# A hybrid decoder layer on one core: modulation tiles issued by GpSimd

## The chip, the cores and the metric

The kernel runs on one core of a Trainium2 chip. The time is the device time of one execution in microseconds (us). TensorE (PE), VectorE (DVE), ScalarE (ACT), GpSimd (POOL) and SyncE (SP) each work through a queue of their own in order; semaphores tie them together. DMAs are issued from such a queue: in the kernel before nearly all of them by SP.

## The reference

One layer of a decoder on 256 tokens with 2048 channels, in f32. What matters here:

```python
mod = jax.nn.silu(c) @ w_ada[l] + b_ada[l]                     # (1, 6*2048), w_ada is 2048 x 12288
shift1, scale1, gate1, shift2, scale2, gate2 = jnp.split(mod[:, None, :], N_MOD, axis=-1)
h = rms_norm(x, norm1_gain[l]) * (1 + scale1) + shift1
x = x + gate1 * mixing_sublayer(h, w_in[l], ...)               # three attention branches behind h @ w_in
h = rms_norm(x, norm2_gain[l]) * (1 + scale2) + shift2
x = x + gate2 * swiglu(h, w_ffn_in[l], w_ffn_out[l])
```

`c` is one vector, so the modulation is a product of a vector with a 100 MB matrix.

## The kernel before

**Precise matmuls.** Every weight tile (`raw`, 128 x 1024 f32, 0.5 MB) is loaded by SP, cast by ACT to a rounded part (`whi`, L148), and DVE subtracts to get the rest (`wlo`, L149). `mm3` (L154 to L156) makes three matmuls of each product. There are four buffers each of `raw`, `whi` and `wlo`.

**The modulation** does not run on TensorE. Tiles of `w_ada` are loaded, and DVE multiplies each by one element of silu(c) per partition (`csil`) and adds it up in `ada` (`ada_mac`: L257 for the first tile of a sum, L259 for the others). At the end TensorE transposes the sums (L309), DVE reduces them (L310), and `finish_columns` (L316, L319) adds the bias and makes shift and scale. `make_h` then makes the two parts of the modulated input (ACT L417, DVE L421 and L424).

**Groups.** The 16 chunks of 128 channels of h are made in four groups (3, 4, 4 and 5 chunks), so that the input projection can start with the first three. While TensorE runs the 13 column blocks of the projection for the chunks of one group, the modulation of the next group is summed up (`ada_group`, 16 tiles for the second and the third group, 32 smaller ones for the fourth). Its tiles take turns in the buffers named in `ADA_TAGS`, which the first group uses too. The gate and second-norm segments follow later, in tiles of 128 x 1024 with buffers `AR0`, `AR1` and others (`ada_segment_steps`, L346).

**The opening** (`first_group`, `load_vectors`). SP issues c, three vectors (gains and the bias of the modulation), three of the first group's `w_ada` tiles (L486, 128 x 2 x 384), the first weight tile, x in four parts, the other thirteen `w_ada` tiles, then weight tiles and the second group's tiles. POOL makes the identity and issues seven small vectors. TensorE runs matmuls whose result nobody uses (`keep_warm`, counts in `WARM`) between its first transposes. DVE adds up the sixteen products, the last one in three pieces; a chain of sum, `finish_columns` and `make_h` for each of the three chunks leads to the first matmuls of the projection.

**The order.** A list scheduler sets the order of the instructions on each engine: it goes by priorities (`prio`), data dependences, buffers and its own estimates of when each engine is free; `tc.issue_after` adds an edge. So a change of the issuing engine also changes orders on the other engines. In every queue, a waiting instruction holds up all that stand behind it.

Of the kernel before, what the change touches and what calls it, by code (L numbers as in the profile page):

```python
# [17 lines left out]
P = 128  # L18
# [5 lines left out]
NB = 512  # L24
# [8 lines left out]
RATE_IN, RATE_MID, RATE_FFN = 0.8, 0.6, 0.4  # L33
DEFER = 4
AHEAD = 4000
WARM = (22, 43, 10, 3)
FIN = 13
GROUPS = ((0, 3), (3, 7), (7, 11), (11, 16))
GLA_LEVELS = (1, 2, 4, 8, 16, 32, 64)
# [27 lines left out]
def trunk(ctx: ExitStack, tc: tile.TileContext, I, out):  # L67
    nc = tc.nc
# [14 lines left out]
    def S(tag, shape, dtype=F32):  # L83
        return slot.tile(shape, dtype, tag=tag, name=nm(tag))

    def small(shape, dtype=F32, bufs=8):
        return sp.tile(shape, dtype, tag="tiny", name=nm("tiny"), bufs=bufs)
# [10 lines left out]
    @contextmanager  # L98
    def prio(offset=AHEAD):

        with tc.high_priority(offset=offset):
            start = tc.cur_priority
            yield
            n = tc.cur_priority - start
        tc.cur_priority += n

    state = {"rate": 0.0}
# [84 lines left out]
    def by_chunk(name):  # L192
        return I[name].rearrange("o (k p) -> (o k) p", p=P)
# [14 lines left out]
    rows = S("H6", [P, P])  # L208
    brow = S("H5", [P, P])
# [1 line left out]
    bada = const.tile([P, 96], F32, name="bada")  # L211

    def load_vectors():
        nc.sync.dma_start(rows[16:32, :], by_chunk("norm1_gain"))
        nc.sync.dma_start(brow[0:96, :], by_chunk("b_ada"))
        nc.sync.dma_start(rows[32:48, :], by_chunk("norm2_gain"))
        with tc.issue_after(made):
            for r, name in (
                (ROW_SBQ, "sb_q_gain"),
                (ROW_SBK, "sb_k_gain"),  # L220
                (ROW_DILQ, "dil_q_gain"),
                (ROW_DILK, "dil_k_gain"),
            ):
                nc.gpsimd.dma_start(rows[r : r + 1, :], I[name])
            nc.gpsimd.dma_start(rows[ROW_GB : ROW_GB + 4, :], by_chunk("b_gla_a"))
            nc.gpsimd.dma_start(rows[ROW_GG : ROW_GG + 2, :], by_chunk("gla_out_gain"))
            nc.gpsimd.dma_start(rows[0:16, :], by_chunk("c"))
# [24 lines left out]
    w_ada = I["w_ada"]  # L252

    def ada_mac(acc, raw, k):
        c = csil[:, k : k + 1]
        if k == 0:
            nc.vector.tensor_scalar(acc, raw, c, None, op0=ALU.mult)  # L257
        else:
            nc.vector.scalar_tensor_tensor(acc, raw, c, acc, op0=ALU.mult, op1=ALU.add)  # L259

    ADA_TAGS = ("T4", "T5", "OS0", "OS1", "OS2", "OD")

    mod1 = const.tile([P, 2, KC], F32, name="mod1")

    def ada_group(k0, k1, tags=ADA_TAGS, between=None):

        n = k1 - k0
        sh, sc = mod1[:, 0, k0:k1], mod1[:, 1, k0:k1]
        count = 0
        pieces = -(-n // 4)  # L270
        for i in range(pieces):
            a = k0 + n * i // pieces
            m = k0 + n * (i + 1) // pieces - a
            w = m * P
            acc = S("ada", [P, 2, w])
            for k in range(KC):
                with prio():
                    raw = S(tags[count % len(tags)], [P, 2, w])
                    nc.sync.dma_start(
                        raw,  # L280
                        w_ada[k * P : (k + 1) * P, : 2 * D].rearrange("p (s c) -> p s c", s=2)[:, :, a * P : a * P + w],
                    )
                    with tc.issue_after(state["macs_after"]) if "macs_after" in state else nullcontext():
                        ada_mac(acc, raw, k)
                count += 1
                if k < KC - 1:
                    yield
            if between is not None:
                between()
            with prio():  # L290
                c = slice(a - k0, a - k0 + m)
                sums = small([P, 2, m])
                for j in range(2):
                    turned_sums(sums[:, j, :], acc[:, j, :])
                finish_columns(sums[:, 0, :], sh[:, c], SEG_SHIFT1, a)
                finish_columns(sums[:, 1, :], sc[:, c], SEG_SCALE1, a, ROW_N1)
            yield
        gains[GROUPS.index((k0, k1))] = (sh, sc)
# [4 lines left out]
    def turned_sums(dst, acc, behind=None):  # L303

        n = dst.shape[1]
        ps = misc_bank([P, n, P])
        for i in range(n):
            with tc.issue_after(behind) if behind is not None else nullcontext():
                nc.tensor.transpose(ps[:, i, :], acc[:, i * P : (i + 1) * P], ident)  # L309
        nc.vector.reduce_sum(dst, ps, axis=AX.X)  # L310
# [12 lines left out]
    def araw(shape, dtype=F32):  # L323
        ring["n"] += 1
        return S(ring["tags"][ring["n"] % len(ring["tags"])], shape, dtype)
# [10 lines left out]
    def ada_segment_steps(acc, seg, done):  # L336


        for k in range(KC):
            for j in range(2):  # L340
                while len(macs) >= len(ring["tags"]):
                    mac()
                raw = araw([P, 2 * NB])
                c0 = seg * D + j * 2 * NB
                with prio():
                    nc.sync.dma_start(raw, w_ada[k * P : (k + 1) * P, c0 : c0 + 2 * NB])  # L346
                macs.append((acc, j, k, raw, done if (k, j) == (KC - 1, 1) else None))
                yield

# [51 lines left out]
    def keep_warm(n):  # L401

        ps = acc_bank()
        for _ in range(n):
            state["warm"] = nc.tensor.matmul(ps, ones_r, wide, start=True, stop=True)
# [26 lines left out]
    A = [None] * 13  # L432
# [42 lines left out]
    def first_group():  # L475


        k0, n = GROUPS[0]
        w = n * P
        tags = tuple(f"A{j}" for j in range(9)) + ADA_TAGS  # L480
        raws = []

        def load(ks):
            for k in ks:
                raw = S(tags[k % len(tags)], [P, 2, w])
                nc.sync.dma_start(raw, w_ada[k * P : (k + 1) * P, : 2 * D].rearrange("p (s c) -> p s c", s=2)[:, :, :w])  # L486
                raws.append(raw)

        load(range(0, 3))
        early.extend(load_weights(w_in, 0, 2, orders[0][0] * NB, ahead=False))  # L490
        split = state["split"]
        load_x()
        load(range(3, KC))
        with tc.issue_after(c_turn.ins):
            keep_warm(WARM[0])
        with tc.issue_after(state["warm"].ins):
            turn_vectors()
        with tc.issue_after(state["row_turn"].ins):
            keep_warm(WARM[1])
        norm1()  # L500
        with tc.issue_after(state["turn"].ins):
            keep_warm(WARM[2])
        acc = S("ada", [P, 2, w])
        for k in range(KC - 1):
            with tc.issue_after(split.ins) if k > 3 else nullcontext():
                ada_mac(acc, raws[k], k)
        sh, sc = mod1[:, 0, 0:n], mod1[:, 1, 0:n]
        chunk = lambda q: slice(q * P, (q + 1) * P)

        def last_mac(q):  # L510
            return ada_mac(acc[:, :, chunk(q)], raws[KC - 1][:, :, chunk(q)], KC - 1)

        last_mac(0)
        last_mac(1)
        behind = state["warm"]
        for q in range(n):
            if q == 0:
                sums = misc_bank([P, 2])
                for j in range(2):
                    with tc.issue_after(behind.ins):  # L520
                        behind = column_sum(sums[:, j : j + 1], acc[:, j, chunk(q)])
            else:
                ps = misc_bank([P, 2, P])
                for j in range(2):
                    with tc.issue_after(behind.ins):
                        behind = nc.tensor.transpose(ps[:, j, :], acc[:, j, chunk(q)], ident)
                sums = small([P, 2])
                with tc.issue_after(state["h_lo"].ins):
                    nc.vector.reduce_sum(sums, ps, axis=AX.X)
            finish_columns(sums[:, 0:1], sh[:, q : q + 1], SEG_SHIFT1, q)  # L530
            finish_columns(sums[:, 1:2], sc[:, q : q + 1], SEG_SCALE1, q, ROW_N1)
            if q == 0:
                with tc.issue_after(state["finish"].ins):
                    last_mac(2)
            make_h(q, sh[:, q : q + 1], sc[:, q : q + 1], True)
            if q == 0:
                with tc.issue_after(state["h_first"].ins):
                    early.extend(load_weights(w_in, 2, n, orders[0][0] * NB, ahead=False))
        with tc.issue_after(behind.ins):
            keep_warm(WARM[3])  # L540
        gains[0] = (sh, sc)

    with prio(30000):
# [687 lines left out]
```

## Time and profile before

| | us |
|---|---|
| Median of 3 runs (lowest, highest) | 1619.66 (1618.76, 1620.27) |
| Profiled execution, its own time | 1621.66 |
| Its span in the trace | 1619.90 |
| PE busy | 1604.0 |
| DVE busy | 1118.7 |
| ACT busy | 796.2 |
| POOL busy | 5.3 |
| Transfers | 395.94 MB, mean 244 GB/s |

Busy times are sums over the span; a busy PE includes the unused matmuls of the opening. The granted clock of TensorE is 1.00 in the whole execution. In the views of the profile a row names the line of the kernel, the engine, the tile written and the tiles read; `SPq` and `POOLq` are the DMA issues of those queues. Lines are those of the kernel before; the changed kernel is one line shorter, so that its later lines stand one earlier.

### The profile page before, as it was taken

The page shows a single profiled execution, that of the slowest core. Times are in us where ns is not written, and L with a number is a line of the kernel's source. Part 1 is how long each engine was busy: PE and PEld are TensorE (multiplying, and loading weights), DVE is VectorE, ACT ScalarE, POOL GpSimd, SP SyncE. Part 2 cuts the span into 40 slices and gives each one's busy share as a digit, 9 for nine tenths or more (in the row PEclk, how much of TensorE's full clock was granted, in tenths as well). Part 3 has the DMA queues.
Part 4 walks back from the last instruction along what each step waited for, and adds up shares of the span by engine and source line. Part 5 has one row for each costly group of instructions (what it writes and reads, how often), then busy time and mean ns, then how long its engine had stood idle before and what let it go on. Part 6 is the DMA issues. An engine that isn't in the chain of part 4 may idle for free.

```text
span 1619.9 us, 19947 instructions
## 1 busy us (share of the span) xinstructions
PE 1604.0 (99%) x7341; PEld 1322.8 (82%) x7341; DVE 1118.7 (69%) x1301; ACT 796.2 (49%) x1116; POOL 5.3 (0%) x14
## 2 busy tenths in 40 slices
PE   8999999999999999999999999999999999999998
PEld 7878888788888878888887888888888888888887
DVE  6889995869888687878657566667655555455453
ACT  5654448764875434444446544444434444433332
POOL 1000000000000000000000000000000000000000
PEclk9999999999999999999999999999999999999999
DMA  9999997865868889888766577888666666666663
GB/s 323 340 328 325 330 307 240 275 215 163 288 213 262 298 297 313 309 298 297 242 192 193 167 242 255 276 266 270 199 194 183 193 184 189 188 206 196 207 205 107
DMA packets 194594, 395.94 MB, mean 244 GB/s; under 512 B 12915, under 2 KB 27929, under 8 KB 194497
## 3 DMA queue, kind: packets, MB, share of 16 engines
q1 hardware_dynamic: 194272, 394.67, 75.1%
q8 instruction: 57, 0.93, 0.2%
q14 instruction: 41, 0.33, 0.1%
q0 software_dynamic: 224, 0.01, 0.0%
HBM read 392.53 MB, written 2.10 MB: 244 GB/s over the span
## 4 chain that ended last, share of the span: by engine, by line
PE 89%; DMA 4%; DVE 3%; ACT 2%; issue 1%; SPq 0%; DVEq 0%; ACTq 0%
PE acc L156 28%; PE acc L155 28%; PE acc L154 28%; DMA raw<-w_in 1%; DVE wlo L149 1%; ACT whi L148 1%; PE misc L742 1%; PE misc L1017 1%; DMA AR<-w_ada 1%; DMA A<-w_ada 1%; DMA OS<-w_ada 1%; DVE ada L259 0%; DMA raw<-w_br_gla 0%; PE misc L309 0%; DMA raw<-w_ffn_in 0%
## 5 line engine op out<-in xcount | busy, mean ns | idle before, releaser
L149 DVE TENSOR_TENSOR wlo<-raw,whi 128x1024 fp32r<-128x1024 f32 (+1 forms) x546 | 651.4, 1197 | 436.5 <-ACT whi L148 434.8
L148 ACT CAST whi<-raw 128x1024 fp32r<-128x1024 f32 (+1 forms) x546 | 562.5, 1033 | 713.8 <-PE acc L156 591.4
L155 PE MATMUL acc<-wlo,H 128*128 128x512 f32 x1576 | 615.4, 390 | 1.7 <-DVE wlo L149 1.5
L154 PE MATMUL acc<-whi,H 128*128 128x512 f32 x1576 | 616.2, 391 | 0.5 <-ACT H L417 0.4
L156 PE MATMUL acc<-whi,H 128*128 128x512 f32 x1576 | 615.5, 391 | 0.4 <-DVE H L424 0.4
L155 PEld LDWEIGHTS acc<-wlo,H 128*128 128x128 f32 x1576 | 296.0, 188 | 62.9 <-DVE wlo L149 2.9
L156 PEld LDWEIGHTS acc<-whi,H 128*128 128x128 f32 x1576 | 295.7, 188 | 63.3 <-DVE H L424 1.8
L154 PEld LDWEIGHTS acc<-whi,H 128*128 128x128 f32 x1576 | 295.9, 188 | 61.3 <-ACT H L417 1.3
L154 PE MATMUL acc<-whi,A 128*128 128x512 f32 x312 | 122.0, 391 | 0.3 <-ACT whi L148 0.3
L155 PE MATMUL acc<-wlo,A 128*128 128x512 f32 x312 | 121.5, 389 | 0.8 <-DVE wlo L149 0.8
L156 PE MATMUL acc<-whi,A 128*128 128x512 f32 x280 | 109.0, 389 | 0.0
L259 DVE SCALAR_TENSOR_TENSOR ada<-AR,csil,ada 128x1024 f32<-128x1024 f32 x59 | 75.1, 1277 | 1.2 <-DMA AR<-w_ada 1.2
L155 PEld LDWEIGHTS acc<-wlo,A 128*128 128x128 f32 x312 | 58.6, 188 | 13.1 <-DVE wlo L149 1.1
L154 PEld LDWEIGHTS acc<-whi,A 128*128 128x128 f32 x312 | 58.6, 188 | 12.7 <-ACT whi L148 0.7
L156 PEld LDWEIGHTS acc<-whi,A 128*128 128x128 f32 x280 | 52.5, 188 | 10.9
L154 PE MATMUL acc<-whi,T 128*128 128x512 f32 x120 | 46.7, 389 | 0.0
L155 PE MATMUL acc<-wlo,T 128*128 128x512 f32 x120 | 46.7, 389 | 0.0
L156 PE MATMUL acc<-whi,T 128*128 128x512 f32 x120 | 46.7, 389 | 0.0
L156 PE MATMUL acc<-whi,OS 128*128 128x512 f32 x112 | 43.6, 389 | 0.0
L259 DVE SCALAR_TENSOR_TENSOR ada<-OS,csil,ada 128x1024 f32<-128x1024 f32 (+2 forms) x33 | 35.6, 1077 | 1.5 <-DMA OS<-w_ada 1.3
L461 ACT COPY A<-acc 128x512 f32<-128x512 f32 x50 | 28.9, 586 | 12.5 <-PE acc L156 11.2
L463 DVE TENSOR_TENSOR A<-A,acc 128x512 f32<-128x512 f32 x48 | 31.5, 682 | 2.0 <-PE acc L156 1.8
(337 smaller groups left out, 1214.8 us busy)
## 6 DMA issues: line engine op xcount, KB each, us to landing
raw<-w_in SPq DMA_DIRECT2D x205, 512.0 KB, 5.0
raw<-w_ffn_in SPq DMA_DIRECT2D x176, 512.0 KB, 3.9
raw<-w_ffn_out SPq DMA_DIRECT2D x88, 512.0 KB, 4.7
AR<-w_ada SPq DMA_DIRECT2D x79, 512.0 KB, 4.8
raw<-w_out SPq DMA_DIRECT2D x32, 512.0 KB, 5.0
KC<-w_ada SPq DMA_DIRECT2D x30, 512.0 KB, 5.1
OS<-w_ada SPq DMA_DIRECT2D x16, 512.0 KB, 6.4
raw<-w_br_gla SPq DMA_DIRECT2D x16, 512.0 KB, 7.0
```

The source lines that it names most:

```text
L148: state["cast"] = nc.scalar.copy(hi[:, :n, :], raw[:, :n, :])
L149: state["split"] = nc.vector.tensor_tensor(lo[:, :n, :], raw[:, :n, :], hi[:, :n, :].bitcast(F32), op=ALU.subtract)
L154: nc.tensor.matmul(ps, lh, rh, start=start, stop=False, skip_group_check=seeded)
L155: nc.tensor.matmul(ps, lh, rl, start=False, stop=False, skip_group_check=seeded)
L156: state["mm"] = nc.tensor.matmul(ps, ll, rh, start=False, stop=stop, skip_group_check=seeded)
L259: nc.vector.scalar_tensor_tensor(acc, raw, c, acc, op0=ALU.mult, op1=ALU.add)
L461: nc.scalar.copy(A[b][:, t, :], pss[t])
L463: nc.vector.tensor_add(A[b][:, t, :], A[b][:, t, :], pss[t])
L742: nc.tensor.matmul(ps[:n, h, L:], at(lhs, h, t)[:, :n], at(rhs, h, t)[:, L:], start=True, stop=True)
L1017: nc.tensor.transpose(ps[:, i, :], src[:, i * P : (i + 1) * P], ident)
```

## The change

All `w_ada` tiles but those of the first group are issued by GpSimd instead of SP. Three vectors of the opening are issued by ScalarE instead of SP. The order of the buffers in `ADA_TAGS` is turned by one place (the first group keeps the old order). The unused matmuls are regrouped, 73 in three groups for 78 in four. The third weight chunk of the first block is cast and split behind the second chunk of h instead of the first.

```diff
-WARM = (22, 43, 10, 3)
+WARM = (22, 38, 13)
...
     def load_vectors():
-        nc.sync.dma_start(rows[16:32, :], by_chunk("norm1_gain"))
-        nc.sync.dma_start(brow[0:96, :], by_chunk("b_ada"))
-        nc.sync.dma_start(rows[32:48, :], by_chunk("norm2_gain"))
+        nc.scalar.dma_start(rows[16:32, :], by_chunk("norm1_gain"))
+        nc.scalar.dma_start(brow[0:96, :], by_chunk("b_ada"))
+        nc.scalar.dma_start(rows[32:48, :], by_chunk("norm2_gain"))
...
-    ADA_TAGS = ("T4", "T5", "OS0", "OS1", "OS2", "OD")
+    ADA_TAGS = ("OD", "T4", "T5", "OS0", "OS1", "OS2")
...
     def ada_group(k0, k1, tags=ADA_TAGS, between=None):
...
                     raw = S(tags[count % len(tags)], [P, 2, w])
-                    nc.sync.dma_start(
+                    nc.gpsimd.dma_start(
                         raw,
                         w_ada[k * P : (k + 1) * P, : 2 * D].rearrange("p (s c) -> p s c", s=2)[:, :, a * P : a * P + w],
                     )
...
     def ada_segment_steps(acc, seg, done):
...
-                    nc.sync.dma_start(raw, w_ada[k * P : (k + 1) * P, c0 : c0 + 2 * NB])
+                    nc.gpsimd.dma_start(raw, w_ada[k * P : (k + 1) * P, c0 : c0 + 2 * NB])
...
     def first_group():
...
-        tags = tuple(f"A{j}" for j in range(9)) + ADA_TAGS
+        tags = tuple(f"A{j}" for j in range(9)) + ADA_TAGS[1:] + ADA_TAGS[:1]
...
             make_h(q, sh[:, q : q + 1], sc[:, q : q + 1], True)
-            if q == 0:
-                with tc.issue_after(state["h_first"].ins):
+            if q == 1:
+                state["casts_after"] = state["h_hi"].ins
+                with tc.issue_after(state["h_lo"].ins):
                     early.extend(load_weights(w_in, 2, n, orders[0][0] * NB, ahead=False))
-        with tc.issue_after(behind.ins):
-            keep_warm(WARM[3])
         gains[0] = (sh, sc)
```

## The prediction

> **What bounds the kernel now.** I read the engine shares and the chain of work first. TensorE is the bound:
>
> ```profile
> PE 1604.0 (99%) x7341; PEld 1322.8 (82%) x7341; DVE 1118.7 (69%) x1301; ACT 796.2 (49%) x1116; POOL 5.3 (0%) x14
> PE 89%; DMA 4%; DVE 3%; ACT 2%; issue 1%; SPq 0%; DVEq 0%; ACTq 0%
> ```
>
> So the time is the moment at which PE's real matmuls start to run without a break, plus a fixed amount of PE work, plus the few stalls behind it. The change can only move the start and the stalls. Next I read the windows (columns: window, length, busy time of PE, PEld, DVE, ACT, POOL, granted clock, DMA share, GB/s); the last three were chosen round the stalls that the timeline shows:
>
> ```profile
> 0.00:10.00 10.00, 7.48 (x23) 5.92 (x23) 2.98 (x10) 1.47 (x2) 4.28 (x13) 1.00 0.66 203
> 10.00:20.00 10.00, 10.00 (x45) 7.84 (x44) 5.17 (x7) 8.45 (x23) 0.00 (x0) 1.00 1.04 385
> 20.00:30.00 10.00, 10.00 (x78) 9.39 (x76) 8.78 (x10) 5.27 (x10) 0.00 (x0) 1.00 1.06 376
> 100.00:150.00 50.00, 50.00 (x223) 41.40 (x222) 47.88 (x50) 19.82 (x20) 0.00 (x0) 1.00 0.96 335
> 270.00:284.00 14.00, 13.03 (x71) 10.64 (x70) 9.49 (x14) 11.27 (x20) 0.00 (x0) 1.00 0.85 280
> 318.00:324.00 6.00, 5.49 (x26) 4.29 (x25) 4.46 (x7) 3.35 (x6) 0.00 (x0) 1.00 0.81 262
> 574.00:584.00 10.00, 8.95 (x38) 6.85 (x38) 6.10 (x8) 4.06 (x4) 0.00 (x0) 1.00 0.89 309
> ```
>
> The opening is limited by transfers: 9.64 MB move in 30 us, in the end at 376 GB/s, and the chain of waits passes through them into the last modulation products of the first group:
>
> ```profile
> 18.10 9.32 DMA OS<-w_ada
> 27.52 1.03 DVE ada L259
> 28.57 1.03 DVE ada L259
> 29.62 1.03 DVE ada L259
> 151.92 0.87 PE misc L309 x8
> ```
>
> The timeline gives the landmarks (start, length, engine):
>
> ```profile
> 1.19 0.41 SPq L214 DMA_DIRECT2D H<-norm_gain  x1
> 2.58 1.46 SPq L486 DMA_DIRECT2D A<-w_ada  x3
> 10.85 1.05 ACT L148 CAST whi<-raw 128x1024 fp32r<-128x1024 f32 x1 [7.85 <-DMA raw<-w_in]
> 23.45 2.07 DVE L259 SCALAR_TENSOR_TENSOR ada<-T,csil,ada 128x768 f32<-128x768 f32 x2
> 30.68 0.88 DVE L259 SCALAR_TENSOR_TENSOR ada<-A,csil,ada 128x256 f32<-128x256 f32 x2
> 37.82 0.75 DVE L257 TENSOR_SCALAR ada<-T,csil 128x1024 f32<-128x1024 f32 x1
> 39.76 0.50 PE L155 MATMUL acc<-wlo,H 128*128 128x512 f32 x1
> 50.09 0.39 PE L156 MATMUL acc<-whi,H 128*128 128x512 f32 x1
> 51.45 0.39 PE L156 MATMUL acc<-whi,H 128*128 128x512 f32 x1
> ```
>
> The first group's sixteenth tile is used at 30.68; 7.14 us later DVE starts the second group's first product (L257), and 1.94 us after that, at 39.76, PE runs on. The last two rows are six matmuls apart: 0.2267 us each.
>
> **The change, part by part.** *Three vectors to ScalarE's queue.* SP's first w_ada issue moves from 2.58 to 1.19: the transfers start 1.39 us earlier.
>
> *AR tiles at the very start.* In the built order two gate tiles (128x1024 f32, 0.524 MB each) stand on POOL ahead of the identity, since nothing holds them there; before, they stood at the 169th place of SP's queue. 1.05 MB at 376 GB/s is 2.8 us in a stretch that is limited by transfers. Together: the sixteenth tile, without anything else, at 30.68 - 1.39 + 2.8 = 32.1. DVE's new order (the first weight split ahead of csil) lets the products begin only behind that weight tile, 10.85 + 1.4 = 12.3, plus 3.1 for cast, split and csil; the backlog is worked off before the fourth tile, so this costs nothing.
>
> *POOL's own queue.* It can issue a tile of the second group as soon as a T or OS buffer is free, that is behind the first group's tenth product (23.45 + 1.05 + 1.4 = 25.9), and 1.4 us later its bytes flow, at 27.3. They then run beside the rest of SP's stream instead of behind it. How POOL's transfers share the engines, two rows bound:
>
> ```profile
> H<-sb_k_gain POOLq DMA_DIRECT2D x1, 0.5 KB, 2.0
> H<-c POOLq DMA_DIRECT2D x1, 8.0 KB, 5.1
> 4.50 0.52 POOL L227 DMA_DIRECT2D H<-c  x1
> ```
>
> An idle fabric lands a POOL transfer in 2.0 us; issued at 4.50 into SP's backlog, 8 KB took 5.1, yet came before the weight tile that SP had issued at 4.08 (used at 10.85). So POOL's tiles neither wait for all of SP's nor pass them. I take half the rate for each. [...]
>
> From 27.3 the first group still lacks (31.1 - 27.3) x 0.376 = 1.4 MB (bytes end about 1 us before 32.1). At half rate that is 7.4 us: the sixteenth tile at 35.7, L257 at 42.9, PE runs on at 44.8. The other path: the new tag order makes the second group's first product use OD, the fifth of POOL's tiles (2.62 MB); DVE takes products and splits in order, so the next weight split waits behind it. Both queues moving 2.62 MB from 27.3 end at 41.2; landed 42.2, PE at 44.1. So 44.8, or **+5.0 us**. Bounds: -1.4 (POOL's tiles and the AR tiles disturb nothing) to +7.5 (SP's stream first, including 0.79 MB of constants that now stand behind the third block's first weight tile, OD last). I take the middle, where the 5.1 us row puts it. The unused matmuls (73 for 78) and the split moved from the second to the third chunk cost nothing: the split leaves one chain of mod and h and enters the next, whose end sets L257.
>
> *The group change.* 477 real matmuls (built order) stand between 39.76 and the L309 row at 151.92: 108.1 us, with 0.9 for eight transposes 148.8. PE lost 3.1 us there, most of it at 84 to 96, where the second group's sums come last. In the new order the first of these transposes stands 49 matmuls (11 us) earlier, so the sums and h lie under other matmuls: **-3.1** (bounds -3.1 and 0).
>
> Does DVE keep up? It works off each product behind a split, in these steps:
>
> ```profile
> 40.26 1.28 DVE L259 SCALAR_TENSOR_TENSOR ada<-T,csil,ada 128x1024 f32<-128x1024 f32 x1
> 41.45 1.82 DVE L149 TENSOR_TENSOR wlo<-raw,whi 128x1024 fp32r<-128x1024 f32 x2
> 43.19 2.60 DVE L259 SCALAR_TENSOR_TENSOR ada<-OS,csil,ada 128x1024 f32<-128x1024 f32 x2
> ```
>
> 1.19 us from start to start for a product, 1.74 for a pair of splits. Up to PE's 751st matmul the new order holds 64 products, the old one 53; by such distances, summed along that order, DVE needs 160.5 us from L257 where PE has 168.3 of work. It keeps up, with less room than before.
>
> *Bytes at the group change.* Before the second group's first pair of weight tiles is complete, 32.6 MB must have landed (opening 9.0, third weight tile and constants 1.05, AR 1.05, 22 products' tiles 11.5, weights 10.0). 9.64 have moved at 28.6 (30 less 1.4), and (32.6 - 9.64) / 0.376 later is 89.7, with landing, product and split 91.7. PE comes there after 215 matmuls and eight transposes, at 44.8 + 49.5 = 94.3. The room of 2.6 us is 1.0 MB, two tiles under way: **+0.7** (0 to 1.4).
>
> *Later stalls.* The three last windows hold 0.97, 0.51 and 1.05 us without PE. They begin at weight tiles that came late:
>
> ```profile
> SPq L136 <- DVE wlo L149: 904.1, 437, 13.2
> SPq L346 <- DVE ada L259: 96.4, 78, 3.8
> 245.28 7.68 DMA raw<-w_in
> 568.25 0.33 SPq L346
> 568.67 6.95 DMA raw<-w_br_gla
> ```
>
> SP's queue stood 96.4 us behind gate tiles, with weights queued behind them; at 568 a weight is issued right behind such a tile. POOL takes these waits, behind which nothing else waits but later gate tiles. Of 2.5 us I take half, **-1.2** (bounds -2.5 and 0), since the splits that free the buffers hold SP nine times as long.
>
> **Sum:** 5.0 - 3.1 + 0.7 - 1.2 = +1.4 us. The profiled execution took 1621.66 (span 1619.90), so 1623.1 by its own time; it lies 2.0 above the median of the runs, and from 1619.66 the forecast is **1621.1**, which is no change within 0.2% (3.2 us, about what a measurement of this kernel can tell). Its own range, the opening between +2 and +6.5: 1618 to 1623.
>
> **Rivals.** *DVE becomes the bound (slower).* This decides if a product costs its whole length and not the distance above:
>
> ```profile
> L259 DVE SCALAR_TENSOR_TENSOR ada<-AR,csil,ada 128x1024 f32<-128x1024 f32 x59 | 75.1, 1277 | 1.2 <-DMA AR<-w_ada 1.2
> ```
>
> With 1277 ns and its like DVE needs 174.5 us to PE's 751st matmul against 168.3: PE stalls 6.1 more, and nothing later gives it back. 5.0 - 3.1 + 6.1 = +8.0: 1627.7. For: DVE is busy 47.88 of 50 us in the window from 100. Against: the start-to-start rows. 0.27, with a worse opening counted here.
>
> *SP keeps its way (faster).* AR tiles out of the way or POOL served in gaps: opening +2.0, the group change -3.1, stalls -2.5: -3.6, 1616.0. For: the 96.4 us of waits that SP loses; against: 376 GB/s leaves no gaps in the opening. 0.17.
>
> *POOL cannot make the tiles (much slower).* Its issue takes 0.52 us for 16 rows; were that by rows, 128 rows of two pieces cost 8. At 4 us each, sixteen tiles take 64 us where PE works 37 (164 matmuls) up to the sums: +27 in the second group alone, 1646 or more. Against: one row and sixteen take POOL the same. 0.06. [...]
>
> *Nothing happens:* the same engines move the same bytes, 1619.7. 0.04.
>
> **Chances.** Forecast 0.46; the others as given. Faster 0.17; same 0.46 + 0.04 = 0.50; slower 0.27 + 0.06 = 0.33. The range reaches from below the faster case to above the DVE case, 1615 to 1629; it leaves out the POOL case and ends of the others.
>
> **What would show it.** Right: the sixteenth tile's product near 35.7, PE running on near 44.8, no gap near the second group's first block, three later stalls halved. Wrong: PE running on before 41 (half shares are wrong), DVE without idle time and PE waiting for wlo from 100 to 220 (DVE), POOL's issues back to back at over 2.5 us (POOL).

## The result, and the profile after

The changed kernel takes 1634.55 us (median of 4 runs, 1634.22 to 1635.86) against 1619.21 for the kernel before (1618.35 to 1620.27): ratio 1.0095, 95% interval [1.0084, 1.0107]. It is 15.3 us slower; the forecast was 1621.1 in a range of 1615 to 1629. The two profiled executions, 1632.5 and 1619.9 us of span, are 12.6 apart.

The page of the changed kernel, engine shares and chain of work:

```profile
PE 1608.2 (99%) x7336; PEld 1326.6 (81%) x7336; DVE 1118.7 (69%) x1301; ACT 795.1 (49%) x1116; POOL 119.5 (7%) x206
PE 89%; DMA 6%; DVE 2%; issue 2%; ACT 1%; SPq 0%; DVEq 0%; ACTq 0%; POOLq 0%
```

DVE is exactly as busy as before (1118.7 us), so it does no more work; the transfers' share of the chain went from 4 to 6%. The windows view (same columns as in the prediction) shows where PE ran less, and that its clock was no longer full:

```profile
30.00:40.00 10.00, 8.56 (x34) 6.27 (x32) 7.06 (x22) 4.05 (x7) 1.44 (x2) 0.83 1.04 387
40.00:50.00 10.00, 6.83 (x24) 5.23 (x23) 6.70 (x7) 4.09 (x7) 2.17 (x3) 0.83 1.02 366
80.00:110.00 30.00, 25.90 (x110) 21.02 (x110) 26.03 (x32) 17.65 (x27) 7.26 (x11) 0.94 1.03 386
344.00:360.00 16.00, 13.77 (x55) 10.84 (x54) 10.89 (x15) 7.98 (x14) 1.58 (x3) 0.89 0.82 280
```

**The opening.** Its timeline in the changed kernel (start, length, engine; in brackets the idle time before and what ended it):

```profile
25.35 0.78 POOL L279 DMA_DIRECT2D T<-w_ada  x1 [18.36 <-DVE ada L259]
31.38 0.88 DVE L259 SCALAR_TENSOR_TENSOR ada<-A,csil,ada 128x256 f32<-128x256 f32 x2 [0.18 <-DMA A<-w_ada]
31.50 0.72 POOL L279 DMA_DIRECT2D OD<-w_ada  x1 [2.25 <-DVE ada L259]
41.55 0.75 DVE L257 TENSOR_SCALAR ada<-OD,csil 128x1024 f32<-128x1024 f32 x1 [2.94 <-DMA OD<-w_ada]
43.49 0.50 PE L155 MATMUL acc<-wlo,H 128*128 128x512 f32 x1 [3.17 <-DVE wlo L149]
44.72 0.63 PE L154 MATMUL acc<-whi,H 128*128 128x512 f32 x1
45.14 0.63 PE L155 MATMUL acc<-wlo,H 128*128 128x512 f32 x1
```

The first group's sixteenth tile is used at 31.38, only 0.7 later than before. What is late is the OD tile: issued at 31.50, used at 41.55, with the next split behind it. PE runs on at 43.49 instead of 39.76. The last two rows are 0.42 apart, where a matmul at full clock takes 0.2267. The first matmuls behind the wait still ran 0.23 apart; the granted clock is 0.5 from 44.28 to 47.69. Such matmuls at half clock are called cold below.

**The change to the second group.** The sums of the second group, and its later h:

```profile
78.32 1.28 DVE L259 SCALAR_TENSOR_TENSOR ada<-T,csil,ada 128x1024 f32<-128x1024 f32 x1
78.58 0.39 PE L155 MATMUL acc<-wlo,H 128*128 128x512 f32 x1
79.51 0.68 DVE L149 TENSOR_TENSOR wlo<-raw,whi 128x512 fp32r<-128x512 f32 x1
80.11 1.27 DVE L259 SCALAR_TENSOR_TENSOR ada<-OS,csil,ada 128x1024 f32<-128x1024 f32 x1
81.44 1.65 PE L309 MATMUL misc<-ident,ada 128*128 128x128 f32 x8 [2.47 <-DVE ada L259]
83.32 0.63 PE L154 MATMUL acc<-whi,H 128*128 128x512 f32 x1
92.06 1.28 DVE L259 SCALAR_TENSOR_TENSOR ada<-OS,csil,ada 128x1024 f32<-128x1024 f32 x1
96.19 0.42 DVE L424 TENSOR_TENSOR H<-scr,H 128x256 fp32r<-128x256 f32 x1
106.53 0.42 DVE L424 TENSOR_TENSOR H<-scr,H 128x256 fp32r<-128x256 f32 x1
107.00 0.73 PE L156 MATMUL acc<-whi,H 128*128 128x512 f32 x2 [2.65 <-DVE H L424]
```

PE comes to the transposes of the sums and waits 2.47 us for the last product. That product does not wait for its tile: it follows the rows before it without idle time. DVE is behind with its queue, busy 16.68 of the 17.40 us from 64.00 to 81.40 (p2, a run below with SP's queue: 14.66). It had begun late, at 41.55 behind the OD tile, and on the way five splits waited 5.1 us together for casts; the casts stood 16.3 us for weight tiles between 38.6 and 81 us (2.9 in p2). Then h of the second group is made slowly: between its second (96.19) and its third (106.53) DVE does products of the third group and splits, and PE waits 2.65 us.

**The segment tiles.** Late in the span the same thing happens once more, with an AR tile:

```profile
345.45 0.53 POOL L346 DMA_DIRECT2D AR<-w_ada  x1 [3.62 <-DMA AR<-w_ada]
351.22 1.28 DVE L259 SCALAR_TENSOR_TENSOR ada<-AR,csil,ada 128x1024 f32<-128x1024 f32 x1 [2.31 <-DMA AR<-w_ada]
354.10 0.91 PE L653 MATMUL misc<-scr,KC 128*128 128x384 f32 x2 [2.23 <-DVE scr L649]
356.09 0.63 PE L155 MATMUL acc<-wlo,H 128*128 128x512 f32 x1
```

A product that waits 2.31 us for its tile stands on DVE ahead of L649, for which PE waits; cold matmuls follow.

To compare kernels I use two numbers from PE's timeline. "PE on" is the start of the seventh L155 matmul, the first with the third weight chunk (39.76 before). "Lost" is what the distances from one real matmul's start to the next have beyond 0.2267 us each, summed from there to 420 us: stalls and cold matmuls, without the usual time of other matmuls that stand between. Both together are 45.3 before (39.76 + 5.5) and 57.8 after (43.49 + 14.3): 12.5 of the 12.6 us between the spans. Over all the kernels below, the two together follow the span to within 1.8 us.

### The profile page after: what moved, and what is told of

It is laid out like the page before. It is cut to its first block, busy times and chain, and to the rows that moved or that the text cites. A ratio compares the mean times of both kernels' runs of the same rounds, so it can differ in the third digit from the quotient of the medians.

```text
span 1632.5 us, 20073 instructions
## 1 busy us (share of the span) xinstructions
PE 1608.2 (99%) x7336; PEld 1326.6 (81%) x7336; DVE 1118.7 (69%) x1301; ACT 795.1 (49%) x1116; POOL 119.5 (7%) x206
## 4 chain that ended last, share of the span: by engine, by line
PE 89%; DMA 6%; DVE 2%; issue 2%; ACT 1%; SPq 0%; DVEq 0%; ACTq 0%; POOLq 0%
PE acc L156 28%; PE acc L154 28%; PE acc L155 28%; DMA raw<-w_in 2%; DMA AR<-w_ada 1%; DMA OD<-w_ada 1%; DVE wlo L149 1%; PE misc L741 1%; PE misc L1016 1%; DVE ada L259 1%; DMA A<-w_ada 1%; ACT whi L148 1%; PE misc L309 0%; DMA raw<-w_ffn_in 0%; PE misc L621 0%
## 5 line engine op out<-in xcount | busy, mean ns | idle before, releaser
L155 PE MATMUL acc<-wlo,H 128*128 128x512 f32 x1576 | 617.5, 392 | 3.5 <-DVE wlo L149 3.5
L155 PEld LDWEIGHTS acc<-wlo,H 128*128 128x128 f32 x1576 | 297.5, 189 | 64.7 <-DVE wlo L149 4.2
L155 PE MATMUL acc<-wlo,A 128*128 128x512 f32 x312 | 121.4, 389 | 0.0
L346 POOL DMA_DIRECT2D AR<-w_ada x79 | 42.1, 533 | 628.2 <-DVE ada L259 249.8
L155 PEld LDWEIGHTS acc<-wlo,A 128*128 128x128 f32 x312 | 58.6, 188 | 12.1
L155 PE MATMUL acc<-wlo,T 128*128 128x512 f32 x120 | 46.7, 389 | 0.0
```

The costliest lines, as they stand in the source:

```text
L155: nc.tensor.matmul(ps, lh, rl, start=False, stop=False, skip_group_check=seeded)
L346: nc.gpsimd.dma_start(raw, w_ada[k * P : (k + 1) * P, c0 : c0 + 2 * NB])
```

## The experiments

Each ratio compares a run with the kernel before as it ran in the same set of runs; its median there lay between 1618.01 and 1619.21 us, so that times of different sets can be compared to about 1 us. In the column on the order, "planned" is the order that the scheduler made for that kernel.

| run | w_ada queue | order on the engines | PE on | lost | time, us | ratio to before [95%] |
|---|---|---|---|---|---|---|
| before | SP | planned | 39.76 | 5.5 | 1619.21 | |
| after | GpSimd | planned | 43.49 | 14.3 | 1634.55 | 1.0095 [1.0084, 1.0107] |
| p1 queue alone | GpSimd | planned | 42.38 | 16.8 | 1637.26 | 1.0110 [1.0095, 1.0125] |
| p2 all but the queue | SP | planned | 38.63 | 4.0 | 1616.87 | 0.9982 [0.9973, 0.9991] |
| p3 segments on SP | groups GpSimd | planned | 42.25 | 16.0 | 1635.04 | 1.0099 [1.0084, 1.0115] |
| p4 groups on SP | segments GpSimd | planned | 40.59 | 9.2 | 1625.19 | 1.0039 [1.0025, 1.0054] |
| p5 | GpSimd | that of p2 | 43.64 | 7.8 | 1624.58 | 1.0032 [1.0021, 1.0044] |
| p6 | SP | that of after | 38.43 | 26.2 | 1642.17 | 1.0151 [1.0132, 1.0170] |
| p7 = p5, AR held | GpSimd | that of p2 | 41.00 | 6.2 | 1621.87 | 1.0016 [1.0006, 1.0025] |
| p8 old unused matmuls | GpSimd | planned | 43.75 | 17.4 | 1637.12 | 1.0116 [1.0097, 1.0134] |
| p9 sums held | GpSimd | planned | 43.12 | 14.1 | 1634.13 | 1.0099 [1.0084, 1.0115] |
| p10 products paced | GpSimd | planned | 46.38 | 9.1 | 1632.97 | 1.0087 [1.0074, 1.0101] |
| p11 = p10, AR held, old tags | GpSimd | planned | 38.98 | 18.7 | 1630.11 | 1.0075 [1.0059, 1.0091] |
| p12 vectors alone | SP | planned | 39.72 | 3.1 | 1617.51 | 0.9992 [0.9983, 1.0000] |
| p13 = p10, behind h | GpSimd | planned | 43.86 | 12.3 | 1631.61 | 1.0077 [1.0062, 1.0092] |
| p14 | GpSimd | VectorE's of p2 | 44.39 | 8.8 | 1627.89 | 1.0052 [1.0037, 1.0067] |
| p15 | GpSimd | TensorE's of p2 | 42.62 | 21.4 | 1639.61 | 1.0125 [1.0108, 1.0142] |
| p16 = p7, T4 first | GpSimd | its own on SP | 38.63 | 7.4 | 1623.45 | 1.0027 [1.0017, 1.0036] |
| p17 products behind h | GpSimd | planned | 43.45 | 10.9 | 1630.38 | 1.0075 [1.0060, 1.0090] |
| p18 = p17, sums held | GpSimd | planned | 43.55 | 11.7 | 1632.93 | 1.0093 [1.0076, 1.0110] |

### Which part of the change

```diff
 p1: before.py, in ada_group and ada_segment_steps:
-    nc.sync.dma_start(raw, w_ada...)
+    nc.gpsimd.dma_start(raw, w_ada...)
 p2: after.py, the same two lines back to nc.sync
 p3: after.py, only the line in ada_segment_steps back to nc.sync
 p4: after.py, only the line in ada_group back to nc.sync
```

> The kernel before with nothing changed but the queue of the modulation tiles: both w_ada issues behind the first group go to GpSimd; vectors, unused matmuls, buffer order and the third split stay as before. Theory (the second queue makes the loss: its tiles run beside SP's weights in a full fabric, and the order that comes with it puts the second group's sums and h among the matmuls): about +10 of the +15.3 us, 1629, with PE stalls at L309 and L424 near 80 and 107 us and one near 350. Rival (the regrouped unused matmuls and the buffer order make it, through cold matmuls in the opening and the late OD tile): 1619 to 1622.

> The changed kernel with both w_ada issues back on SP; vectors on ScalarE, 73 unused matmuls, buffer order and third split as changed. Theory (the queue makes the loss): 1618 to 1621, within 0.15% of before. Rival (regrouped unused matmuls and buffer order): 1625 or more, with the granted clock under 1 between 30 and 50 us.

> The changed kernel with only the segment tiles (AR, KC, KD; L346) back on SP, the group tiles (L279) still on GpSimd. Theory: the opening and group stalls stay (PE on at about 43, stalls at 70, 81, 107), the stall near 352 with its cold matmuls goes (2.6 + 1.3 us): 1630. Rival (the two AR tiles at the very start make the opening late): opening back to within 1 us of before, 1625 or less.

> The changed kernel with only the group tiles (L279) back on SP, the segment tiles on GpSimd. Theory: no stalls at 70, 81 and 107, PE on near 40 to 42; the stall near 352 stays: +3 to +6, 1622 to 1625. Rival (AR tiles at the very start and regrouped unused matmuls make the opening's loss): PE on at 43 or later and 1628 or more.

The queue alone makes more than the whole loss, and the rest of the change is a small gain: p2 is 2.3 us faster than before. p2 came out below its expected range, p1 above its 1629; p4 came out as its theory said, with PE on at 40.59 and a stall of 1.88 us at 346. The two queues' parts don't add up: against p2 the segment tiles alone cost 8.3 us (p4), the group tiles alone 18.2 (p3), both 17.7. In p3 the stall near 354 is gone, as expected, but the loss at the group change grew by as much (12.8 us between 60 and 130 where the changed kernel has 7.4), so its time is not the 1630 that I expected.

### Queue against order

In the built order, moving the issue to GpSimd also rewrites what TensorE, VectorE and ScalarE do when: the second group's sums stand 164 matmuls in, where p2 has them after 208. The kernels p5, p6, p14 and p15 separate the two. Every instruction of a pinned engine is tied behind the one that precedes it in the other kernel's built order; the text of the kernel is otherwise the same. SP and GpSimd are not pinned, and the scheduler orders them anew. In p5 GpSimd's DMA issues stand exactly as in the changed kernel and SP's in 605 of 607 places; in p6 SP's are at another place than in p2 in 88 of 799 cases:

```diff
     with tile.TileContext(nc) as tc:
         trunk(tc, aps, out)
+        pin(nc, tc)      # for each engine listed: the other kernel's order
...
+        for a, b in zip(order, order[1:]):
+            tc.add_manual_dep(ins[b], ins[a].name, NoSync)
 p5:  after.py, PE, DVE, ACT pinned to p2's order
 p6:  p2, PE, DVE, ACT pinned to after.py's order
 p14: after.py, DVE alone pinned to p2's order
 p15: after.py, PE alone pinned to p2's order
```

> The changed kernel, all its w_ada tiles on GpSimd as changed, but TensorE, VectorE and ScalarE are made to take their instructions in exactly the order that they have in the kernel with everything but the queue (p2_all_but_queue); buffers, queues and bytes stay as changed. Theory A (the order decides: the planner thinks that GpSimd's tiles come earlier and puts products, sums, h and L649's work ahead of splits, and the chip's transfers do not): stalls at L309 near 81, at H L424 near 107 and at scr L649 near 354 go, the opening's loss of 3 to 5 us against p2 stays: 1620 to 1623. Theory B (the second queue itself delays the weights): stalls move to other places but stay, 1629 or more.

> The kernel with everything but the queue (p2_all_but_queue, all w_ada tiles on SP), but TensorE, VectorE and ScalarE take their instructions in exactly the order of the changed kernel. Theory A (the order decides): stalls at L309 near 81, at L424 near 107 and near 352 show with SP's queue too: 1624 to 1632. Theory B (the queue decides): no such stalls, 1616 to 1619.

> The changed kernel, all w_ada tiles on GpSimd; VectorE alone is made to take its instructions in the order of p2_all_but_queue, TensorE's and ScalarE's order is left to the planner. Theory A2 (VectorE's order, products ahead of splits and h, is the loss): 1623 to 1627, most of the 10 us that p5 won. Rival A1 (where TensorE takes the sums decides): 1630 or more.

> The changed kernel, all w_ada tiles on GpSimd; TensorE alone is made to take its instructions in the order of p2_all_but_queue, VectorE's and ScalarE's order is left to the planner. Theory A1 (where TensorE takes the sums decides): 1623 to 1627. Rival A2 (VectorE's order): 1630 or more, with waits for wlo or for h L424 behind products that wait for their tiles.

This table separates the two:

| | order of p2 | order planned for GpSimd |
|---|---|---|
| tiles on SP | 1616.87 (p2) | 1642.17 (p6) |
| tiles on GpSimd | 1624.58 (p5) | 1634.55 (after) |

With the order of p2 held, the second queue costs 7.7 us; with the queue held on GpSimd, the new order costs 10.0. These two are clean. The new order on SP costs 25.3, but p6 differs from p2 in SP's own issues too, so that this number, and the 7.6 us by which GpSimd's queue beats SP's in the new order, hold more than one thing. Theory A holds for the larger part, though p5 came out 1.6 us above the time that I gave it and p6 10 above, with no wait for h near 107 but one of 4.56 us for wlo at 104.88. In p6, with SP's queue, PE waits for the same sums and DVE for OS tiles (timeline, and the groups view with the idle time behind the second bar):

```profile
81.06 1.33 PE L309 MATMUL misc<-ident,ada 128*128 128x128 f32 x5 [5.42 <-DVE ada L259]
L259 DVE SCALAR_TENSOR_TENSOR ada<-OS,csil,ada 128x1024 f32<-128x1024 f32 (+2 forms) x31 | 33.3, 1075 | 17.0 <-DMA OS<-w_ada 16.9
```

In p2 the last product of the second group comes at the same time as in the changed kernel (79.89 against 80.11), but PE asks for the sums after it, and the fourth h is made at 92.91:

```profile
79.89 1.28 DVE L259 SCALAR_TENSOR_TENSOR ada<-OS,csil,ada 128x1024 f32<-128x1024 f32 x1
81.42 1.04 PE L309 MATMUL misc<-ident,ada 128*128 128x128 f32 x8
92.91 0.42 DVE L424 TENSOR_TENSOR H<-scr,H 128x256 fp32r<-128x256 f32 x1
```

So the new order doesn't bring the sums sooner; it only makes PE and DVE stand in line for them sooner. p14 and p15 ask whose order it is. With TensorE in the order of p2 and VectorE planned (p15), the time is 5.1 us worse still, because h comes late:

```profile
103.85 0.80 PE L156 MATMUL acc<-whi,H 128*128 128x512 f32 x1 [5.86 <-DVE H L424]
```

With VectorE in the order of p2 (p14), 6.7 of the 10.0 us are won back; p14 lies between its two expectations, 0.9 above the first. But p14 is not VectorE's order alone: with it given, the scheduler put TensorE's instructions as in p2 in 7308 of 7336 places (as in the changed kernel in 7094), the second group's sums after 200 matmuls. So TensorE's order does not mend it without VectorE's; whether VectorE's would without TensorE's no run shows.

### The opening

```diff
 p7:  p5, and the segment tiles behind the last group tile on GpSimd's queue
+    with tc.issue_after(state["ada_dma"].ins):
         nc.gpsimd.dma_start(raw, w_ada[..., c0 : c0 + 2 * NB])
 p16: p7 with ADA_TAGS = ("T4", "T5", "OS0", "OS1", "OS2", "OD"),
      pinned to the order of p2 with these tags
 p8:  after.py with WARM = (22, 43, 10, 3) and the closing keep_warm
 p12: before.py with the three vectors on nc.scalar
```

> As p5_queue_with_old_order, and the segment tiles are queued on GpSimd behind the last group tile, so that the two AR tiles no longer stand at the very start. Theory (1.05 MB at 376 GB/s in a full fabric): the opening is 2 to 2.8 us earlier than in p5, all else equal, 1618 to 1621. Rival (the two tiles move beside constants and cost nothing): the same time as p5 within 0.7 us.

> As p7_old_order_AR_held, with the buffer order of before in addition (T4 first; the pinned order is that of the same kernel on SP with this buffer order). Theory (what p7 still loses in the opening is the OD tile, issued fifth and used first; VectorE waited 1.67 us for it): PE runs on 1.5 to 2.5 us earlier, 1619.5 to 1620.5. Rival (the second queue's tiles delay whatever comes): 1621 to 1623 as p7.

> The changed kernel with the unused matmuls of before (22, 43, 10 and the closing 3). Theory (the cold matmuls between 33.9 and 37.3 lie ahead of a wait for wlo that ends at 43.5 whatever PE does, so they cost nothing): 1634 to 1635.5, the same within 0.1%, with or without cold rows. Rival (the missing closing matmuls let the clock fall, and that costs): 1630 to 1631.5.

> The kernel before with only the three vectors issued by ScalarE. Theory (SP's first w_ada tile leaves 1.39 us earlier, and PE runs on by that much earlier): 1617.5, 0.09% faster, PE running on near 38.4. Rival (the transfers limit the opening, and the same bytes come first by another queue): the same as before within 0.5 us, and the 2 us of p2_all_but_queue come from its other parts.

p7: the two AR tiles at the start cost 2.64 us of "PE on" (43.64 to 41.00) and 2.7 of the time; its time is 0.9 above the expected range, as p5's was 1.6 above its own. p16: with the OD tile out of the way PE runs on 2.37 earlier, at 38.63, exactly where p2 does. But the time is no better than p7's, and 0.5 above its rival's range. In p2 nothing is lost up to 60 us; in p16 3.8 us are, in waits for weights:

```profile
45.92 0.50 PE L154 MATMUL acc<-whi,H 128*128 128x512 f32 x1 [0.40 <-ACT whi L148]
49.06 0.49 PE L154 MATMUL acc<-whi,H 128*128 128x512 f32 x1 [0.97 <-ACT whi L148]
50.32 0.50 PE L155 MATMUL acc<-wlo,H 128*128 128x512 f32 x1 [0.77 <-DVE wlo L149]
```

The windows view shows the two kernels moving the same bytes at the same rate there, PE getting less of what it needs in p16 (p2's row first):

```profile
33.00:62.00 29.00, 27.81 (x120) 21.86 (x120) 26.45 (x36) 18.93 (x29) 0.00 (x0) 1.00 1.00 352
33.00:62.00 29.00, 25.14 (x101) 17.95 (x101) 21.58 (x31) 15.38 (x24) 5.78 (x8) 1.00 0.98 350
```

The fabric (the 16 DMA engines together) is full in both (shares 1.00 and 0.98), and in p16 GpSimd's queue moves 5.31 of the 10.15 MB, so that tiles that DVE uses later take places of weights that PE waits for (the shares of the two queues are in the last section). Something else stands ahead of weights there too: with the group tiles gone from SP's queue, SP issues constants and small weights of the attention branches (0.79 MB) at 25 to 33 us, in the changed kernel, p5, p7 and p16 alike, where before and p2 issue them at 235 to 251. At 376 GB/s that is 2.1 us, an estimate. No run holds the constants back, so how p16's 3.8 us divide between the two stays open.

p8 refutes the rival that the missing closing matmuls are the loss: PE runs on at 43.75, 0.26 later than in the changed kernel, and the time is not better. I had expected the same time within 0.1%; the median is 2.6 us higher (the intervals overlap), all of it at the group change, where 14.4 us are lost between 60 and 130. p1 and p3 lose 12.5 and 12.8 there. Why shifts of a microsecond move this between 7 and 14 us is open.

p12 came out at the 1617.5 that I expected (its interval reaches to no gain at all), not for the reason that I gave. The sixteenth tile is used earlier (29.06 against 30.68), but PE runs on at 39.72: it is still busy with the unused matmuls, whose last group but one ends just as it takes the first sum (31.35), and DVE waits 2.01 us for that. What p12 gains are the stalls between 73 and 94 us, 2.4 us before and none in p12. In p2, with five unused matmuls fewer, PE takes the first sum at 30.25 and runs on at 38.63.

### Mending the order by single edits

```diff
 p9:  after.py
-    turned_sums(sums[:, j, :], acc[:, j, :])
+    turned_sums(sums[:, j, :], acc[:, j, :], state["mm"].ins)
 p10: after.py
-    with tc.issue_after(state["macs_after"]) if "macs_after" in state else nullcontext():
+    with tc.issue_after(state["split"].ins):
         ada_mac(acc, raw, k)
 p13: both issue_after of p10's two lines
 p11: p10, and the segment tiles held as in p7, and ADA_TAGS as before
 p17: after.py
-    with tc.issue_after(state["macs_after"]) if "macs_after" in state else nullcontext():
+    with tc.issue_after(state["h_lo"].ins):
         ada_mac(acc, raw, k)
 p18: p17 and p9
```

> The changed kernel, all w_ada tiles on GpSimd, with one edit: the transposes of a later group's sums (L309) are queued on TensorE behind the last matmul traced before them, so that they stand 216 matmuls in, not 164 (before: 213); the products on VectorE stay as early as the changed order has them. Theory A1 (the early sums and h are the loss): the stalls near 81 (2.6 us) and 107 (2.8) go: 1627 to 1630. Theory A2 (the products standing ahead of splits are the loss): the same time moves into waits for wlo, 1632 or more.

> The changed kernel, all w_ada tiles on GpSimd, with one edit: each product of a later group is queued on VectorE behind the split traced last before it, as the segment products already are; the sums then stand 200 matmuls in by themselves. Theory A (the planned order is the loss, and pacing the products mends it): like p5_queue_with_old_order, 1623 to 1626, without stalls over 1 us at L309 and L424. Rival (only the exact order of p2_all_but_queue does it): 1630 or more.

> As p10_products_paced, but the second group's products are also kept behind the first group's last h on VectorE, as the changed kernel keeps them (p10 let the first product, which waited for its OD tile, stand ahead of that h). Theory (one product that waits for its tile ahead of h costs the whole wait): PE's stall of 4.5 us at 42.8 in p10 becomes one of about 2 for wlo, PE runs on near 43.6 where p10 did at 46.4: 1630 to 1631. Rival (the wait only changes its name): 1632.5 to 1633.5 as p10.

> As p10_products_paced, with the segment tiles queued on GpSimd behind the last group tile (no AR tiles at the very start) and the buffer order of before (T4 first, so that the first product of the second group doesn't use the fifth tile issued). Theory (AR tiles at the start cost 2.7 us, as p7 showed against p5; the OD tile about 1.7, VectorE's wait for it there): 1619 to 1621.5. Rival (the second queue's tiles delay the weights whichever comes first): 1623 or more.

> The changed kernel, all w_ada tiles on GpSimd, with one edit: the products of each group stand on VectorE behind the last h of the group before (L424), not among its h. Theory (five products and seven splits of the third group that stand ahead of the second group's third h make the stall of 2.8 us at 107): that stall goes, the one at L309 near 81 stays: 1630 to 1632. Rival (the late h waits for weights or sums anyway): 1634 or more.

> As p17_products_behind_h, and the sums are held as in p9_sums_held (216 matmuls in). Theory (p9 won 2.6 us at L309 and lost them at h, because products stood ahead of h): both stalls go, 1626 to 1629. Rival (sums at 216 come too late for h whatever stands on VectorE): a wait for h of 2 us or more near 98 stays, 1631 or more.

p9: the stall at L309 is gone, and waits for h of 1.80 us at 98.5 and 1.44 at 102.9 take its place, with half clock from 100.05 to 106.88. The time is theory A2's, but the waits are for h and not for wlo. p10: its rival holds in time, and p13 shows half of why. p10 let the first product, which waits for OD, stand ahead of the third h; PE waited 4.37 us for that at 42.8. With the product behind h again PE runs on at 43.86 rather than 46.38, but only 1.4 of these 2.5 us arrive at the end, and a wait of 2.97 us at L309 stays in both (3.67 in p10). p11 is inconclusive on its parts: its runs lie between 1628.35 and 1636.08; its time is the rival's in any case. p17 is the one edit that pays: products of the third group behind the second group's last h, and the fourth h is made at 98.76 where the changed kernel made it at 109.47; no stall at 107, and 4.2 us gained over the changed kernel (2.65 were that stall; by the ratios, each against its own set, it is about 3). p18, both edits together, is worse than p17: with the sums held, h comes late whatever stands on DVE (waits of 1.32 us at 98.5 and 0.82 at 101.4). None of them comes near p5, which has the whole order of p2.

Faster than both kernels is p2, which keeps everything but the second queue: 0.9982 [0.9973, 0.9991].

## Why the prediction was wrong

The sum had four terms; DVE and the clock stood in it at nothing. Against each stands what the profiles and runs show.

- **Opening, +5.0: measured +3.7**, near, but partly by luck. The path that was to decide failed: the sixteenth tile was used at 31.38, not 35.7, because the first packet of GpSimd's group tiles came at 29.6 and not at 27.3, when SP's tiles were nearly through. The "other path", the OD tile with a split behind it, decides; it was given 44.1 and came at 43.49, though with other shares of the fabric than the half that I had estimated (SP's queue got 0.41 of 1.17 MB from 33 to 36 us), see below. The AR tiles were right (2.8 foreseen, 2.6 to 2.7 by p7 against p5). The OD tile costs 2.4 of "PE on", which did not arrive in the time (p16). The vectors do bring the first group's products forward, but that doesn't reach "PE on" by itself (p12): the unused matmuls, costed at nothing, were its limit.
- **Cold matmuls: not foreseen.** They cost 1.6 us behind the wait at 43.49, 1.1 behind L309 and 1.3 behind the stall at 354 (these two are counted again in the terms below). Those between 33.9 and 37.3 cost nothing, since the wait for wlo ends later: p8 has none there and runs on no sooner.
- **Group change, -3.1: measured +5.0.** This is the step that failed. Lost time between 60 and 130 us went from 2.4 to 7.4. I took the sums' earlier place in the order as a gain, as if the products would come earlier too. They didn't: the last one came at 80.11, as with SP's queue (79.89), because it stands on DVE behind splits and the late OD tile, and DVE had no idle time left before it. PE then waited 2.47 us for the sums and 2.65 for an h that stood behind the next group's products.
- **DVE keeps up: right only over the whole stretch.** DVE's busy time did not change, and with the order of p2 the same work on the same queue loses 7.8 us and not 14.3. I compared DVE's capacity with PE's up to the 751st matmul, and asked neither whether DVE would be done by the sums, at the 164th (it was not: 16.68 of 17.40 us busy ahead of them), nor in which order it would wait. The rival "DVE becomes the bound" is wrong as a rate over the stretch; at the sums it is what happened.
- **Bytes at the group change, +0.7:** PE has no wait for them; its waits there are for sums and h. Late weight tiles show one step back, as the 16.3 us that casts stood.
- **Later stalls, -1.2: measured +1.8.** From 130 to 300 us the lost time fell from 1.3 to 0.2, as foreseen. From 300 to 420 it rose from 1.8 to 5.0 by the stall at 354. That goes with the order planned on VectorE for segment tiles from GpSimd: p6 has it too, 1.95 us at 363 with SP's queue, and p2, p3, p5, p7, p14 and p16 don't. From 420 to 600 it is 3.4 and 3.1.

SP's 96.4 us of waiting for products did vanish; the waits view now has them, much longer, on GpSimd, where they hold up nothing but later tiles:

```profile
SPq L136 <- DVE wlo L149: 1125.1, 488, 13.2
POOL AR L346 <- DVE ada L259: 249.8, 51, 39.0
```

The rival "GpSimd cannot make the tiles" is refuted: its issues take 0.72 and 0.53 us.

```profile
L279 POOL DMA_DIRECT2D OS<-w_ada x29 | 20.9, 722 | 47.5 <-DVE ada L259 45.2 <-DVE mod L316 2.3
L346 POOL DMA_DIRECT2D AR<-w_ada x79 | 42.1, 533 | 628.2 <-DVE ada L259 249.8 <-DVE ada L257 246.3 <-DVE T L259 101.4
```

What the change costs, by the 2x2 table: -2.3 (all but the queue), +7.7 (the queue in the old order, 2.7 of it the AR tiles, and with it the constants that SP now issues early), +10.0 (the order that was planned for it). These make up the 15.3 us by construction, each being the step from one measured kernel to the next.

## What to carry to other kernels

Where a planner writes the order, moving a transfer to another queue also rewrites the order of every engine that uses it; compare the built orders and ask, for each instruction that moved forward, whether its data will be there, for whatever is queued behind it waits too (here the split behind the product that stood 2.94 us for its OD tile). Separate the two on the chip by pinning the order: here the queue cost 7.7 us with the order held, and the order planned for it another 10.0. Check too what moves up in the queue that was relieved: here it was 0.79 MB of constants. In a fabric that was full already (share 1.00 in p2 from 33 to 62 us), the second queue brought no bytes (350 GB/s in p16 against 352); it only let tiles that are needed later go ahead of those that are needed now.

## What the hardware showed that I had not expected

**From 33 to 39 us the two queues moved about equal packets, not equal bytes.** The queue rows of the transfer view, changed kernel, 33 to 36 us and then 36 to 39 (packets, MB, share of 16 engines):

```profile
q0 software_dynamic: 216, 0.76, 66.4%
q1 hardware_dynamic: 217, 0.41, 37.6%
q0 software_dynamic: 205, 0.77, 67.1%
q1 hardware_dynamic: 203, 0.39, 35.9%
```

GpSimd's queue and SP's get about as many packets each, but GpSimd's have a mean of 3.5 KB (0.76 MB by 216) and SP's 1.9 KB, so SP's get a third of the bytes, 0.41 of 1.17 MB in 3 us. GpSimd's queue runs dry at times: it issued an OD tile at 42.60, after 9.66 us of waiting for a product of DVE (L257), and from 42.79 to 44.03 it shows no packet. Over 33 to 62 us as a whole the two move about the same, 5.04 and 5.12 MB. Between 25.35, where GpSimd issued its first tile of the second group, and 29.6 us no packet of its queue shows, while SP's earlier tiles fill the engines (share 104.2% from 25 to 28.5 us). The half of the bytes that I had estimated for each queue was wrong for the opening.

**Half clock came in stretches of 3.41 us that lie on one grid, and not behind every gap.** After the gaps that ended at 43.49 (3.17 us), 81.44 (2.47) and 354.10 (2.23) matmuls run 0.43 us apart within a stretch of 3.41 us; after the one that ended at 107.00 (2.65) they don't. The granted clock of the changed kernel is 0.5 in stretches of 3.41 us that begin at 34.04, 44.28, 81.82 and 354.89: 3, 11 and 80 times 3.413 us apart, so they lie on one grid. The windows of that grid just ahead of these four hold 1.43, 2.63, 2.47 and 2.23 us without PE work; the gap before 107.00 is cut by the border at 105.72 into 1.37 and 1.29. In this trace no other window of the grid between 5 and 1600 us holds more than that 1.37, and the clock is 1.00 in the windows that follow them. The kernel before holds at most 1.05 us in a window, with the grid laid from its one half-clock stretch, at 1618.78, and runs at 1.00 up to there. Why half clock followed these four windows and no other, these two traces do not show.
